# A two-layer decoder trunk on one core: layer 0's gate sums all on VectorE, all 256-column softmax scalings on ScalarE, and a new order of all instructions

## The chip, the cores and the metric

The kernel runs on one core of a Trainium2 chip. The core has five engines that matter here: TensorE (PE, with its weight loads PEld), VectorE (DVE), ScalarE (ACT), GpSimd (POOL) and SyncE (SP), which issues most DMA transfers. Each engine works through its own queue of instructions in order, and waits on semaphores for the others. The metric is the time of one execution in microseconds (us). Three runs of the kernel before had a median of 307.33 us (306.77 to 308.2).

## The reference

The reference is a trunk of two layers over 256 tokens of width 1024, in fp32. A vector `c` sets shift, scale and gate of each layer:

```python
c_act = jax.nn.silu(c)
for layer in range(DEPTH):
    ada = jnp.einsum('bd,de->be', c_act, w_ada[layer]) + b_ada[layer]
    shift, scale, gate = jnp.split(ada, 3, axis=-1)
    h = rms_norm(x, norm_g[layer]) * (1.0 + scale[:, None, :]) + shift[:, None, :]
    ...
        y = even_mixer(h, w_in_even[i], w_out_even[i], ...)    # layer 0
    ...
        y = odd_mixer(h, w_in_odd[i], w_out_odd[i], cos, sin)  # layer 1
    x = x + gate[:, None, :] * y
return rms_norm(x, final_g)
```

Layer 0 has two groups of eight heads of width 64: A attends within a window of 128 tokens with a sink for each head, B adds three gated branches (compressed keys, selected blocks, window). At 256 tokens all blocks of B are selected and the window covers everything, so both of those branches are plain causal attention with their own keys and values. The compressed keys and values come from blocks of 32 tokens through a small network. Layer 1 has sixteen heads of causal attention. Each output is multiplied by a SiLU gate path before the output projection.

## The kernel before

**Two steps.** The code first records all operations, with what each depends on, and issues none. `Plan.issue` then issues the 3102 operations in the order of the table `ORDER` at the head of the file. Each engine's queue is the part of that list that belongs to it. All instructions of the recorded part so carry the line of `issue`, L251 in the profile, and are told apart by the names of their tiles.

**Projections.** Weights are loaded by SyncE into a ring of five `raw` tiles of 1 MB (128 partitions x 2048 fp32). ScalarE casts 512 columns at a time to fp32r, the high part `whi`, and VectorE subtracts to get the low part `wlo`. Three products make one fp32 product (`mm3`): high by high, high by low, low by high, into a bank `ps_pj`. The input is split the same way (`hhi`, `hlo` for layer inputs, `ghi`, `glo` for the output projection).

**The sums for shift, scale and gate** (`ada_...`) are products of one row vector with 1024 x 3072 weights a layer, and there are two ways for a piece of 512 columns. With a `"v"` in `SS_ON`, `G0_ON` or `G1_ON`, VectorE does it (`ada_sums`): the weights of four k-tiles fill a `raw` tile, VectorE multiplies each with a per-partition scalar from `cz` and adds it up in `acc`, 128x512, eight operations from two tiles, and one product with `ones` sums over the partitions and broadcasts. With a `"p"`, TensorE does it (`ada_rows`), 256 columns at a time: eight products, 32 columns of stationary `cz` each, in the four column groups of the array, then a copy by ScalarE into `asb` and a product with `selbc` that sums the groups and broadcasts. Either way the last step for the gate is an addition into `gate` on VectorE. `ada_gate` chooses:

```python
if n == 2:
    T.matmul(pc, ones, a, start=True, stop=True)
else:
    T.matmul(pc[:, :256], selbc, ada_rows(ada_tile(l, (16 + h, 17 + h))), start=True, stop=True)
gs = gate[:, h * P : (h + 2 * n) * P]
V.tensor_tensor(gs, pc[:, : 256 * n], gs, ALU.add)
```

The bytes from memory are the same either way: 2 MB for 512 columns.

**Attention of layer 0.** `attn_four` takes two pairs of heads (or the two branches of one pair of B): scores of 128 queries by 128 or 256 keys into `ps_s`; on VectorE the masked minimum of the negated scores into `sm` (or a spare part of `bigA`) and `mn`; on ScalarE the exponential with its sum into `den`; on VectorE the reciprocal `rc`; then a scaling of each tile by `rc`, transposes on TensorE, a copy `pT` on ScalarE and the products with the values into `ps_o`. There are six such calls: two for A (`a_quad`) and four for B (`b_pair`). In each, four scalings have 256 columns and four have 128. `ON_ACT` names those (pair, head, tile) that ScalarE does:

```python
if (n, i, t) in ON_ACT:
    A.mul(sms[i][:, a:b], sms[i][:, a:b], rc[:, n, i, t : t + 1])
else:
    V.tensor_scalar(sms[i][:, a:b], sms[i][:, a:b], rc[:, n, i, t : t + 1], None, op0=ALU.mult)
```

**Compress.** The network of the compressed keys and values has 16 products of 32 stationary columns each for k and for v, in the four column groups; their order is that of `ORDER`.

**What sets the order around the change.** The jobs of gate 0 and of layer 1's shift and scale are recorded between the attention calls (`fill`), but where they run is set by `ORDER` alone: the table was written by a search, and no planner runs with the kernel. The five `raw` tiles tie the order together, since SyncE loads into a tile only when the last reader of its former content is done: ScalarE and VectorE for a weight, VectorE for sums of kind `"v"`, TensorE for those of kind `"p"`.

Of the kernel before, what the change touches and what calls it, by code (L numbers as in the profile page):

```python
# [25 lines left out]
G0_ON = "vp"  # L26
# [3 lines left out]
ON_ACT = ((0, 1, 1), (1, 1, 1))  # L30
# [7 lines left out]
0 3 1 8 44 10 4 92 11 37 6 2 12 40 13 90 5 14 89 524 15 93 36 45 16 38 1006 87 17 18 19 57 96 20 88 21 91 58 47 59 22  # L38
23 41 94 72 60 42 7 24 25 39 95 26 61 27 73 28 74 106 29 30 76 75 31 62 97 77 48 63 78 49 32 105 51 64 33 65 98 152 79
34 153 67 52 82 80 50 35 81 107 108 109 110 111 112 113 114 115 116 117 53 118 66 119 120 121 122 123 124 125 126 127  # L40
128 129 130 131 132 133 134 135 136 137 138 83 139 55 68 140 69 84 99 70 150 141 142 144 100 143 151 101 146 168 180
56 102 85 148 174 147 175 169 103 186 71 181 149 165 104 171 86 183 145 172 213 154 166 184 163 224 177 159 164 178
225 179 161 187 214 170 176 157 185 162 192 223 167 173 226 189 216 182 195 227 188 198 215 210 207 204 155 211 228
201 219 205 193 199 160 218 229 230 231 232 233 234 158 235 236 237 238 239 240 241 242 243 244 245 246 156 247 248
190 249 202 217 256 250 200 208 209 222 258 251 191 252 257 203 220 260 194 196 259 253 212 197 206 261 264 293 275
262 281 254 221 267 278 282 255 296 273 323 263 290 271 283 274 276 265 287 269 324 335 294 305 272 284 325 291 279
336 288 280 326 292 268 285 286 308 295 334 309 337 297 314 289 298 266 333 320 315 338 321 317 306 328 322 339 310
302 303 327 304 277 340 311 318 270 341 342 343 344 345 346 347 348 349 329 350 525 360 351 352 299 330 307 353 361
364 354 300 301 331 355 312 356 365 313 357 319 332 316 358 366 397 362 369 398 427 394 367 368 431 400 388 389 359
385 377 382 432 395 391 386 428 375 399 363 387 371 390 430 376 383 392 373 401 378 402 429 424 433 384 412 396 413  # L50
379 526 393 434 418 415 523 380 435 381 409 425 683 436 406 407 403 940 374 437 438 439 440 441 442 443 444 445 446
370 447 448 372 421 449 419 450 426 458 408 416 809 451 414 452 460 422 410 411 453 417 461 420 462 404 464 454 423
496 459 478 473 490 484 463 471 405 475 455 487 479 472 469 488 476 467 465 480 474 491 456 497 466 485 498 468 477
520 489 521 470 502 492 545 499 457 486 936 514 549 503 504 508 500 550 501 530 535 509 547 510 546 493 522 529 515
494 532 548 516 527 495 533 481 599 538 482 483 531 601 505 534 528 600 511 506 543 602 517 507 537 544 512 603 551
557 513 610 614 938 552 553 536 554 611 555 935 558 690 559 612 556 615 937 605 616 542 617 541 563 606 564 565 618
560 613 561 566 562 686 567 568 604 575 569 518 619 691 519 620 624 621 607 622 576 570 577 623 687 578 579 571 580
625 572 633 587 688 588 589 634 590 573 684 574 632 581 591 582 583 608 592 685 626 627 628 540 629 636 810 637 655
638 654 639 584 585 631 656 586 593 630 635 594 595 640 596 597 598 657 646 641 663 642 647 643 662 644 661 648 649
650 645 689 651 692 693 694 539 695 670 658 659 669 939 696 697 664 698 660 941 699 700 811 652 701 702 665 653 666  # L60
703 676 814 704 705 943 706 971 707 668 708 667 709 710 944 46 711 712 975 1011 742 945 743 744 745 942 746 947 946
951 950 752 955 954 748 959 958 948 949 974 952 953 749 973 956 957 1047 960 961 750 972 755 1169 671 816 770 771 772
675 773 1170 1034 962 774 747 672 778 673 43 963 776 812 713 964 780 714 674 715 965 716 751 717 815 718 753 977 976
980 984 966 979 983 677 777 988 978 678 982 987 986 981 754 813 985 990 989 991 756 967 757 817 679 992 680 719 720
721 681 993 968 758 1041 779 994 759 868 969 995 869 1042 782 870 871 996 781 970 997 1255 1003 998 783 1001 1004 1002
999 1747 760 775 761 1000 762 1005 818 1048 819 1008 1007 722 784 723 872 820 1009 1013 785 873 724 1012 1010 876 763
1049 821 1056 822 1057 765 823 725 874 824 726 786 1014 880 878 727 877 1015 787 793 896 1016 897 898 899 879 728 1050
904 825 1017 902 826 729 906 827 1018 900 828 730 764 829 908 830 1051 831 881 1058 832 1019 1043 731 766 767 768 1044
732 733 833 769 1020 903 1106 1045 1107 1108 1109 1052 1110 788 1116 789 875 790 834 54 734 1114 1059 1111 1060 882
1021 1112 835 791 1061 883 1022 885 909 907 1132 792 1133 1134 1046 1135 905 794 901 1138 795 1378 796 1062 1117 836  # L70
910 837 1136 1023 682 1053 1113 735 838 839 1242 1063 840 797 911 841 1064 918 1243 1024 1115 913 842 1065 884 891 843
1025 844 736 1066 1137 912 845 737 1171 846 1067 847 848 1256 886 887 890 888 1140 849 850 1139 1026 851 852 1068 1142
738 919 853 854 1257 855 889 1069 739 856 1070 1054 1172 857 858 892 893 1143 894 609 1027 1055 1177 1178 1141 1179
1180 740 1028 1391 798 799 1118 895 1173 800 1390 801 1258 802 803 1185 804 1119 1029 741 805 1260 914 915 916 1030
859 1071 1264 1183 917 1072 1265 1073 1181 1186 1074 1075 1174 1266 920 1127 921 922 860 1031 1182 861 1187 1462 862
863 1267 1184 1259 864 1268 1377 1269 1076 1188 1077 1032 1270 1461 865 1033 1271 923 1272 1035 1078 1175 1262 1121
806 1036 1037 1261 1038 1039 1203 1204 1144 1205 1176 1206 1209 924 925 926 1211 927 1145 928 1120 929 1153 1392 930
931 1213 1040 1246 1244 1247 1245 1147 1250 807 1248 1207 1251 1249 1263 866 1314 1315 1393 1316 1210 1317 1480 867
1122 1474 1123 1124 1079 1273 1080 1189 1125 1126 1081 1082 1394 1083 1212 1084 1274 1085 1086 1252 1128 1318 1129
1130 1320 1275 1276 1087 1146 1131 1088 1152 1253 1395 1321 1148 1149 1150 1208 1089 1324 1090 1482 1277 1151 1278  # L80
1190 1279 1322 1280 932 1091 1475 1214 1092 1154 1155 1093 1323 1254 1281 1282 1156 1463 1340 1157 1341 1342 1343 1215
1325 1382 1380 1379 1386 1348 1501 1384 1381 1344 1385 1383 1346 1319 1464 1158 1347 1159 1481 1160 1161 1349 1191
1162 1350 1163 1198 1164 1216 1165 1192 1351 1166 1502 1167 1387 1396 1397 1465 1398 1224 1399 1197 1193 1194 1326
# [1273 lines left out]
```

## Time and profile before

| what | value |
|---|---|
| median of three runs | 307.33 us (306.77 to 308.2) |
| the profiled execution, its whole time | 307.55 us |
| its span, from the first to the last instruction | 305.4 us |
| TensorE (PE) busy | 294.5 us, 96% |
| VectorE (DVE) busy | 258.4 us, 85% |
| ScalarE (ACT) busy | 184.3 us, 60% |
| TensorE's granted clock, mean | 0.997 |

The profile is one execution. The busy time of an engine is the union of its records, which overlap a little on VectorE and more on TensorE, so the price of an operation within a full queue is read from one start to the next. The clock column is 1.00 in all stretches that are used below, so no time in them hangs on it. Where a wait is named, the name on the right is what came last.

### The profile page before, as it was taken

The page shows a single profiled execution, that of the slowest core. Times are in us where ns is not written, and L with a number is a line of the kernel's source. Part 1 is how long each engine was busy: PE and PEld are TensorE (multiplying, and loading weights), DVE is VectorE, ACT ScalarE, POOL GpSimd, SP SyncE. Part 2 cuts the span into 40 slices and gives each one's busy share as a digit, 9 for nine tenths or more (in the row PEclk, how much of TensorE's full clock was granted, in tenths as well). Part 3 has the DMA queues.
Part 4 walks back from the last instruction along what each step waited for, and adds up shares of the span by engine and source line. Part 5 has one row for each costly group of instructions (what it writes and reads, how often), then busy time and mean ns, then how long its engine had stood idle before and what let it go on. Part 6 is the DMA issues. An engine that isn't in the chain of part 4 may idle for free.

```text
span 305.4 us, 6362 instructions
## 1 busy us (share of the span) xinstructions
PE 294.5 (96%) x2331; PEld 252.0 (83%) x2331; DVE 258.4 (85%) x703; ACT 184.3 (60%) x483; POOL 11.3 (4%) x36
## 2 busy tenths in 40 slices
PE   8899999999999999999999999999999999999990
PEld 8777788997789787888877899999789989877890
DVE  1388999998899999999989778598857999997783
ACT  3476147876679778882547854264647646873630
POOL 6000000002000000000001000000000000000011
PEclk9999999999999999999999999999999999999998
DMA  8999999986956979489899292968098493151003
GB/s 240 355 364 372 387 402 372 332 261 194 337 194 197 320 260 329 139 246 339 259 274 329 61 328 63 366 206 290 0 277 276 144 298 113 52 225 71 0 9 128
DMA packets 60669, 71.82 MB, mean 235 GB/s; under 512 B 2712, under 2 KB 52320, under 8 KB 60640
## 3 DMA queue, kind: packets, MB, share of 16 engines
q1 hardware_dynamic: 60032, 70.90, 70.1%
q10 hardware_dynamic: 448, 0.48, 0.4%
q8 instruction: 18, 0.29, 0.4%
q0 software_dynamic: 160, 0.05, 0.3%
q14 instruction: 11, 0.09, 0.1%
HBM read 70.38 MB, written 1.05 MB: 234 GB/s over the span
## 4 chain that ended last, share of the span: by engine, by line
PE 84%; ACT 4%; DMA 4%; DVE 3%; issue 2%; SPq 0%; POOL 0%; POOLq 0%; ACTq 0%; DVEq 0%
PE ps_pj L251 49%; PE ps_s L251 12%; PE ps_m L251 8%; PE ps_pt L251 7%; PE ps_o L251 7%; DMA raw<-in_w_in_even_dram 2%; DMA xs<-in_x_dram 2%; ACT whi L251 2%; DVE wlo L251 1%; ACT t L251 1%; DVE xs L251 1%; DVE t L251 1%; ACT bigA L251 1%; SPq L251 0%; ACT hhi L251 0%
## 5 line engine op out<-in xcount | busy, mean ns | idle before, releaser
L251 ACT CAST whi<-raw 128x512 fp32r<-128x512 f32 (+1 forms) x132 | 74.7, 599 | 28.8 <-PE ps_pj L251 17.2
L251 DVE TENSOR_TENSOR wlo<-raw,whi 128x512 fp32r<-128x512 f32 (+1 forms) x116 | 74.0, 659 | 8.9 <-ACT whi L251 8.7
L251 PE MATMUL ps_pj<-hhi,whi 128*128 128x256 f32 x256 | 68.0, 286 | 0.0
L251 PE MATMUL ps_pj<-hhi,wlo 128*128 128x256 f32 x256 | 67.8, 286 | 0.0
L251 PE MATMUL ps_pj<-hlo,whi 128*128 128x256 f32 x256 | 67.3, 283 | 0.0
L251 PEld LDWEIGHTS ps_pj<-hhi,whi 128*128 128x128 f32 x256 | 46.5, 188 | 1.1 <-issue 0.3
L251 PEld LDWEIGHTS ps_pj<-hhi,wlo 128*128 128x128 f32 x256 | 46.3, 188 | 0.6 <-issue 0.3
L251 PEld LDWEIGHTS ps_pj<-hlo,whi 128*128 128x128 f32 x256 | 46.3, 188 | 0.1
L251 DVE SCALAR_TENSOR_TENSOR acc<-raw,cz,acc 128x512 f32<-128x512 f32 x42 | 31.3, 745 | 0.3
L251 ACT ACTIVATE sm<-sm,mn 128x256 f32<-128x256 f32 (+1 forms) x58 | 26.0, 450 | 6.5 <-DVE mn L251 6.4
L251 PE MATMUL ps_pj<-whi,hhi 128*128 128x512 f32 (+2 forms) x72 | 26.0, 375 | 0.8 <-ACT hhi L251 0.8
L251 DVE SCALAR_TENSOR_TENSOR wlo<-raw,whi 128x512 fp32r<-128x512 f32 x32 | 21.2, 686 | 5.1 <-ACT whi L251 5.1
L251 PE MATMUL ps_pj<-wlo,hhi 128*128 128x512 f32 (+2 forms) x72 | 25.3, 377 | 0.0
L251 PE MATMUL ps_pj<-whi,hlo 128*128 128x512 f32 (+2 forms) x72 | 25.0, 369 | 0.0
L251 PE MATMUL ps_pj<-whi,ghi 128*128 128x512 f32 (+1 forms) x56 | 20.8, 375 | 0.0
L251 PE MATMUL ps_pj<-wlo,ghi 128*128 128x512 f32 (+1 forms) x56 | 20.5, 372 | 0.0
L251 ACT COPY pT<-ps_pt 128x384 f32<-128x384 f32 x25 | 11.9, 476 | 14.2 <-PE ps_pt L251 14.2
L251 PE MATMUL ps_pj<-whi,glo 128*128 128x512 f32 (+1 forms) x56 | 20.1, 365 | 0.0
L251 PEld LDWEIGHTS ps_pj<-whi,hhi 128*128 128x128 f32 x72 | 13.4, 188 | 3.5 <-ACT hhi L251 1.4
L251 PE MATMUL ps_pt<-ta,sm 128*128 128x128 f32 x87 | 15.7, 276 | 0.0
L251 DVE TENSOR_TENSOR t<-ps_pj,tb 128x512 f32<-128x512 f32 (+2 forms) x22 | 12.0, 586 | 3.4 <-PE ps_pj L251 3.4
L251 PEld LDWEIGHTS ps_pj<-wlo,hhi 128*128 128x128 f32 x72 | 13.3, 189 | 1.9 <-DVE wlo L251 0.2
(231 smaller groups left out, 613.2 us busy)
## 6 DMA issues: line engine op xcount, KB each, us to landing
raw<-in_w_in_odd_dram SPq DMA_DIRECT2D x16, 1024.0 KB, 7.6
raw<-in_w_ada_dram SPq DMA_DIRECT2D x28, 512.0 KB, 5.7
raw<-in_w_in_even_dram SPq DMA_DIRECT2D x8, 652.0 KB, 7.0
raw<-in_w_in_even_dram SPq DMA_DIRECT2D x5, 1024.0 KB, 9.0
t<-in_w_ada_dram SPq DMA_DIRECT2D x16, 256.0 KB, 6.0
raw<-in_w_out_even_dram SPq DMA_DIRECT2D x4, 1024.0 KB, 5.4
raw<-in_w_out_odd_dram SPq DMA_DIRECT2D x4, 1024.0 KB, 6.3
qT<-in_w_ada_dram SPq DMA_DIRECT2D x12, 256.0 KB, 7.2
```

The lines of the kernel that those rows point to most:

```text
L251: self.ops.append(dict(key=eng.key, deps=deps, fn=lambda: getattr(real, name)(*args, **kw)))
```

## The change

Three things differ. `G0_ON` goes from `"vp"` to `"vv"`: the second half of layer 0's gate is summed by VectorE. `ON_ACT` goes from two entries to four: in all six calls of `attn_four`, ScalarE does all four scalings of 256 columns, so that twelve move there from VectorE. And `ORDER` is another list, of 3090 operations.

```diff
-G0_ON = "vp"
+G0_ON = "vv"
...
-ON_ACT = ((0, 1, 1), (1, 1, 1))
+ON_ACT = ((0, 0, 1), (0, 1, 1), (1, 0, 1), (1, 1, 1))
...
-3093 3094 3095 3068 3097 3096 3098 3100 3099 3101
...
```

On SyncE's list, the loads of both halves of `x` now come first, and the narrow piece (384 columns) of the first weight tile comes behind the first pieces for layer 0's sums; further on, loads are shuffled, with the same bytes in all. The tiled products of v's compress network and those of layer 1's shift and scale stand in pairs of column groups (0 1 0 1 ... 2 3 2 3, and 1 3 1 3 0 2 0 2 in one of the latter two); before, k's stood so, v's not. TensorE's list has 189 changes between fp32 and fp32r, where it had 209.

On TensorE, behind the products of probabilities and values (`ps_o`) of an early quad of layer 0, the list before has the first of the two row products of the gate's second half (`raw_103,cz`, eight products), and scores (`ps_s`) and projections (`ps_pj`) around it:

```order
L251 MATMUL ps_o_96<-pT_128,vb 64x256
L251 MATMUL ps_o_96<-pT_129,vb 64x256
L251 MATMUL ps_o_96<-pT_128,vb 64x128
L251 MATMUL ps_o_96<-pT_129,vb 64x128
L251 MATMUL ps_m_67<-raw_103,cz 32x256 x8
L251 MATMUL ps_s_90<-kTb,qT_97 128x128
L251 MATMUL ps_s_91<-kTb,qT_97 128x128
L251 MATMUL ps_s_90<-kTb,qT_97 128x256
L251 MATMUL ps_s_91<-kTb,qT_97 128x256
L251 MATMUL ps_pt_83<-ta,sm_124 128x128 x3
```

The changed list has there one product of the summed rows with `ones`, between the transposes (`ps_pt`) of two heads:

```order
L250 MATMUL ps_pj_94<-hhi,wlo_114 128x256
L250 MATMUL ps_pj_93<-hhi,wlo_113 128x256
L250 MATMUL ps_pj_94<-hhi,whi_110 128x256
L250 MATMUL ps_pt_83<-ta,sm_124 128x128 x3
L250 MATMUL ps_m_67<-acc_105,ones 128x512
L250 MATMUL ps_pt_83<-ta,sm_125 128x128 x3
L250 MATMUL ps_s_90<-kTb,qT_97 128x128
L250 MATMUL ps_s_91<-kTb,qT_97 128x128
L250 MATMUL ps_s_90<-kTb,qT_97 128x256
L250 MATMUL ps_s_91<-kTb,qT_97 128x256
```

The row products and the products with `selbc` are gone, and the one with `ones` waits for `acc_105`, VectorE's last multiply-add of that gate half.

On VectorE, the same sums stand in the middle of softmax calls. `ISA` is the masked minimum, `acc_105` the sum; `raw_103` and `raw_100` are the two loads of this gate half. The changed list:

```order
L250 TENSOR_SCALAR sm_125<-sm_125,rc_140 128x128
L250 SCALAR_TENSOR_TENSOR acc_105<-raw_100,cz,acc_105 128x512
L250 TENSOR_TENSOR t_89<-t_89,dc_160 128x16x16
L250 RECIPROCAL rc_138<-den_135 128x4
L250 SCALAR_TENSOR_TENSOR acc_105<-raw_100,cz,acc_105 128x512
L250 ISA sm_123,mn_132<-ps_s_91,tb 128x128
L250 ISA mn_132 128x1
L250 SCALAR_TENSOR_TENSOR acc_105<-raw_100,cz,acc_105 128x512
L250 ISA sm_123,mn_132<-ps_s_91,tb 128x256
L250 ISA mn_132 128x1
L250 SCALAR_TENSOR_TENSOR acc_105<-raw_100,cz,acc_105 128x512
L250 TENSOR_SCALAR sm_126<-sm_126,rc_140 128x128
```

In the list before, this place has the sums of layer 1's shift and scale (`raw_101`), and a scaling of 256 columns (`sm_126`):

```order
L251 TENSOR_SCALAR sm_124<-sm_124,rc_140 128x128
L251 TENSOR_SCALAR acc_105<-raw_101,cz 128x512
L251 ISA sm_123,mn_132<-ps_s_91,tb 128x256
L251 ISA mn_132 128x1
L251 TENSOR_SCALAR sm_126<-sm_126,rc_140 128x256
L251 ISA bigA,mn_132<-ps_s_90,tb 128x128
L251 ISA mn_132 128x1
L251 TENSOR_TENSOR wlo_113<-raw_104,whi_109 128x512
L251 SCALAR_TENSOR_TENSOR acc_105<-raw_101,cz,acc_105 128x512
L251 SCALAR_TENSOR_TENSOR oT<-oT,ps_pj_93 128x512
L251 RECIPROCAL rc_138<-den_135 128x4
L251 TENSOR_SCALAR sm_125<-sm_125,rc_140 128x128
```

The four multiply-adds from `raw_100` now stand among the minima of a pair of heads, two of them between the minima of one head, and the 256-column scaling is no longer in the queue.

On ScalarE, the same softmax calls, where `sm_...<-sm_...,rc_...` is a scaling and `pT` a copy of transposed tiles. Before:

```order
L251 COPY pT_128<-ps_pt_83 128x384
L251 ACTIVATE bigA,den_135<-bigA,mn_132 128x128
L251 ACTIVATE sm_125<-sm_125,rc_140 128x256
L251 ACTIVATE bigA,den_135<-bigA,mn_132 128x128
L251 ACTIVATE bigA,den_135<-bigA,mn_132 128x256 x2
L251 COPY pT_129<-ps_pt_83 128x384
L251 CAST whi_109<-raw_104 128x512
L251 ACTIVATE sm_127<-sm_127,rc_140 128x256
```

And in the changed list:

```order
L250 COPY pT_128<-ps_pt_83 128x384
L250 ACTIVATE sm_123<-sm_123,rc_139 128x256
L250 ACTIVATE sm_125<-sm_125,rc_140 128x256
L250 ACTIVATE sm_124<-sm_124,rc_140 128x256
L250 ACTIVATE bigA,den_135<-bigA,mn_132 128x128
L250 COPY pT_129<-ps_pt_83 128x384
L250 ACTIVATE sm_126<-sm_126,rc_140 128x256
L250 ACTIVATE bigA,den_135<-bigA,mn_132 128x128
L250 CAST whi_109<-raw_104 128x512
L250 CAST ghi<-oT 128x512
L250 ACTIVATE sm_127<-sm_127,rc_140 128x256
```

Two scalings have become five within ten instructions, three of them in a row; the cast `whi_109` behind them makes the high part of a weight.

## Rows read from the trace of the kernel before

**Rows 1.** The page's first part (busy time, share of the span and instructions of each engine).
```profile
PE 294.5 (96%) x2331; PEld 252.0 (83%) x2331; DVE 258.4 (85%) x703; ACT 184.3 (60%) x483; POOL 11.3 (4%) x36
```

**Rows 2.** The page's fourth part, the chain of work that ended last, by engine.
```profile
PE 84%; ACT 4%; DMA 4%; DVE 3%; issue 2%; SPq 0%; POOL 0%; POOLq 0%; ACTq 0%; DVEq 0%
```

**Rows 3.** The view by stretches: from and to, length, then busy time and instructions of PE, PEld, DVE, ACT and POOL, TensorE's granted clock, DMA share, GB/s. The second to the fourth stretch run from the first softmax operation on VectorE over the last score stage and the last gated product of layer 0 to the first low part of layer 1's input.
```profile
16.00:64.00 48.00, 46.80 (x329) 39.64 (x330) 43.76 (x93) 28.99 (x69) 0.00 (x0) 1.00 1.06 370
...
71.60:90.00 18.40, 18.18 (x176) 14.48 (x178) 16.27 (x72) 12.50 (x45) 0.62 (x2) 1.00 0.83 267
90.00:142.90 52.90, 52.90 (x461) 42.79 (x458) 52.42 (x184) 42.09 (x133) 0.00 (x0) 1.00 0.77 249
142.90:163.10 20.20, 20.20 (x109) 15.63 (x108) 18.84 (x41) 9.91 (x20) 0.94 (x3) 1.00 0.93 291
163.10:284.00 120.90, 120.90 (x982) 107.90 (x981) 100.73 (x254) 72.09 (x179) 0.67 (x1) 1.00 0.57 187
```

**Rows 4.** The view of waits, VectorE alone, in the three stretches from 71.6 to 163.1 us, one after the other: the waiting tile, what it waited for, us in total, times, longest.
```profile
DVE sm L251 <- PE ps_s L251: 0.8, 1, 0.8
DVE hx L251 <- ACT sm L251: 0.7, 1, 0.7
DVE hg L251 <- ACT th L251: 0.3, 1, 0.3
...
DVE sm L251 <- PE ps_s L251: 0.2, 1, 0.2
...
DVE t L251 <- PE ps_s L251: 0.6, 1, 0.6
DVE shs L251 <- PE ps_m L251: 0.4, 1, 0.4
```

**Rows 5.** The chain of waits from 103 to 122 us, in order of time: start, us, what. `ps_m` x2 is first the product with `ones` over 512 columns (104.83), then the broadcast product of one gate part (112.73); `ps_m` x16 are the two row products of the gate's second half.
```profile
104.83 0.86 PE ps_m L251 x2
...
108.43 1.00 PE ps_m L251 x16
...
112.73 0.43 PE ps_m L251 x2
...
115.98 1.01 PE ps_m L251 x16
```

**Rows 6.** The timeline of TensorE at 84 us: start, us, line, operation, out<-in, tile, elements. `ps_pj` products are fp32r, those of `w2v` fp32.
```profile
84.26 0.39 PE L251 MATMUL ps_pj<-hhi,whi 128*128 128x256 f32 x2
84.49 0.28 PE L251 MATMUL ps_pj<-hlo,whi 128*128 128x256 f32 x1
...
84.74 0.36 PE L251 MATMUL ps_pj<-hhi,wlo 128*128 128x256 f32 x1
84.94 0.33 PE L251 MATMUL ps_m<-w2v,hr 128*128 128x64 f32 x2
```

**Rows 7.** The timeline of VectorE in two places: gate or shift sums and a softmax call.
```profile
88.60 0.48 DVE L251 TENSOR_SCALAR acc<-raw,cz 128x512 f32<-128x512 f32 x1
89.12 1.54 DVE L251 SCALAR_TENSOR_TENSOR acc<-raw,cz,acc 128x512 f32<-128x512 f32 x2
90.58 0.28 DVE L251 CUSTOM_DVE_ANT_0 sm<-ps_s,tb 128x128 f32<-128x128 f32 x1
...
92.04 0.35 DVE L251 TENSOR_SCALAR bigA<-bigA,rc 128x256 f32<-128x256 f32 x1
92.31 0.28 DVE L251 TENSOR_SCALAR sm<-sm,rc 128x128 f32<-128x128 f32 x1
...
102.39 0.75 DVE L251 SCALAR_TENSOR_TENSOR acc<-raw,cz,acc 128x512 f32<-128x512 f32 x1
103.06 0.17 DVE L251 TENSOR_SCALAR dc<-dc 128x16 f32<-128x16 f32 x1
```

**Rows 8.** The view by operation and shape, VectorE from 64 to 145 us: busy time, mean ns of one, idle before. The additions into the gate.
```profile
L251 DVE TENSOR_TENSOR gate<-ps_m,gate 128x256 f32<-128x256 f32 x2 | 0.8, 412 | 0.0
L251 DVE TENSOR_TENSOR gate<-ps_m,gate 128x512 f32<-128x512 f32 x1 | 0.7, 658 | 0.0
```

**Rows 9.** ScalarE: by operation and shape over the span (the copy behind a row product, and from the page's fifth part the copy of transposed tiles, whose last number is the idle time before it and its releaser), and two rows of its timeline, a scaling and what follows.
```profile
L251 ACT COPY asb<-ps_m 128x256 f32<-128x256 f32 x4 | 1.5, 365 | 2.1 <-PE ps_m L251 2.1
...
L251 ACT COPY pT<-ps_pt 128x384 f32<-128x384 f32 x25 | 11.9, 476 | 14.2 <-PE ps_pt L251 14.2
...
85.45 0.49 ACT L251 ACTIVATE sm<-sm,rc 128x256 f32<-128x256 f32 x1
85.85 0.49 ACT L251 ACTIVATE bigA<-bigA,mn 128x256 f32<-128x256 f32 x1
```

**Rows 10.** The timeline of TensorE: the compress products of k and what follows them, then those of v and what follows.
```profile
71.63 2.82 PE L251 MATMUL ps_m<-raw,t 128*32 128x256 f32 x32
74.38 0.48 PE L251 MATMUL ps_s<-kTb,qT 64*128 64x128 f32 x3
...
77.02 2.84 PE L251 MATMUL ps_m<-raw,t 128*32 128x256 f32 x32 [0.19 <-issue]
79.79 0.44 PE L251 MATMUL ps_pt<-ta,t 128*128 128x128 f32 x2
```

**Rows 11.** The view of waits, SyncE's DMA queue over the span: us in total, times, longest.
```profile
SPq L251 <- DVE wlo L251: 68.9, 16, 8.3
SPq L251 <- DVE acc L251: 37.0, 9, 13.6
```

248 rows, old and new, of the table ORDER are left out of this document.

## The prediction

> **What bounds the kernel now.** I read the page's sums first: TensorE is busy 294.5 of 305.4 us, VectorE 258.4, ScalarE 184.3 [rows 1]. The chain of waits agrees, with 84% of it on TensorE and 4% or less on anything else [rows 2]. That share is an average, so I then cut the span into the stages that the change touches: the loads up to 64 us, then layer 0's attention from the first softmax operation on VectorE (71.6 us) to the last gated product (142.9 us), and the output projection up to the first low part of layer 1's input (163.1 us) [rows 3]. The columns to read are the busy times of PE and DVE. TensorE has no gap to speak of from 71.6 to 163.1. VectorE is nearly as full: 52.42 of 52.90 us in the middle stretch, and 87.53 of 91.50 over the three (16.27, 52.42 and 18.84). So two engines stand side by side, and VectorE's whole reserve there is 2.13 + 0.48 + 1.36 = 3.97 us. ScalarE has 27 us free over the same three stretches. Behind 163.1 us VectorE has 20 us of reserve, and nothing there is edited but the order.
>
> The waits of VectorE name 3.0 of those 3.97 us [rows 4]: three are for scores or projections from TensorE (0.8, 0.2, 0.6), one for layer 1's shift product (0.4), and two for ScalarE in the small compress chain (0.7, 0.3). A shorter list on TensorE can close the first kind, but not the last.
>
> **The change, part by part.** *Gate sums off TensorE.* The second half of the gate leaves two row products of eight tiled multiplications each. On the chain they stand as 1.00 and 1.01 us, each with nothing around it [rows 5]. With them go two broadcast products of 0.43 each, and one ones-product over 512 columns comes, like the one that took 0.86: even. TensorE: -2.0 us.
>
> *Fewer changes between fp32 and fp32r on TensorE.* I counted them in the two lists: 209 before, 189 after. Within a run of fp32r products, two took 0.23 from the start of the first to the start of what follows (84.26 to 84.49), so 0.12 each; a single one between two fp32 products took 0.20 [rows 6]. That is 0.08 for one change. Twenty times 0.08 is 1.6 if every change costs that, 0.8 if only the entry into one kind does; I take 1.3. TensorE's stream is then 3.3 us shorter, with 2.8 and 3.6 as ends.
>
> *Gate sums onto VectorE.* They add one scaling and seven multiply-adds of 128x512. Records overlap on VectorE, so I take starts, not durations: 0.52 from the scaling (88.60) to the next start, 0.73 each for the two multiply-adds behind it (1.46 from 89.12 to 90.58), 0.67 for another (102.39 to 103.06) [rows 7]. With 0.69 they come to 4.8 + 0.5 = 5.3. Two gate additions of 0.41 become one of 0.66, which is -0.2 [rows 8].
>
> *Softmax scalings off VectorE.* Six calls of four heads move two 256-column scalings each: twelve. Start to start one takes 0.27 (92.04 to 92.31) [rows 7]: -3.2. A rope addition over 256 columns and a small copy also leave this stretch in the new order, -0.4. VectorE's list from the first softmax to layer 1's first low part: 5.3 - 0.2 - 3.2 - 0.4 = +1.5 us.
>
> *Onto ScalarE.* The same scaling there is 0.49 long, 0.40 from start to start (85.45 to 85.85) [rows 9]. Twelve are +4.8, and two copies of 0.37 go: +4.1. The 27 us free hide it in sum. What could show is position: the third fence of the change has five scalings within ten instructions of ScalarE's queue, and behind a late one wait transposed copies and casts, for which TensorE waits. If one pile of three stood in the open, 1.2 us would be lost. In the trace of before it is ScalarE's copies of transposed tiles that wait for TensorE, 14.2 us over the span [rows 9], so I take 0.2 and keep 1.2 for the range.
>
> *Tiled products in pairs.* The compress products of k stand in pairs of column groups before already, those of v do not (groups 1 0 0 0 3 3 0 2 2 3 ...). From their start to the next kind of product they took 2.75 and 2.77 us [rows 10]: nothing is to be had, and I put 0. The eight shift-and-scale products of layer 1 go the other way, from a turn over four groups to pairs in one of their two visits: 1.00 for eight products in such turns [rows 5] against 1.38 for eight in pairs, half of 2.75, so up to +0.4 on TensorE, in a stretch where it has company. I put 0.1 of it into the net. The Trainium skill, TensorEngine Tiling (Array Packing), section Key Properties under Tiling Modes, says that tiles operate independently and that different ones can load weights and multiply in parallel. By it v's order, with five neighbours in one group, should have been slower than k's pairs by some of those five (an estimate from the rows: 5 x 0.17, up to 0.9 us); rows 10 show 0.02, so the measurement decides, and by the rule TensorE's stream would be -4.2 instead of -3.3, with the same limit from VectorE.
>
> *The start.* The order of the first loads changes, the bytes do not, and the stage up to 64 us runs on them: a DMA share of 1.06 at 370 GB/s [rows 3]. A piece of 256 KB more or less ahead of the first product is 0.7 us either way; I take 0.
>
> *Sum.* TensorE alone would end the three stretches 3.3 us earlier, at 88.2 instead of 91.5. VectorE cannot: 87.53 busy plus 1.5 is 89.0, so with no idle time left the gain is 2.5. Idle time will be left: the waits for ScalarE and for the shift product (0.7 + 0.3 + 0.4) stay, and with the two lists now equally long neither can run ahead to cover the other's order. In before, VectorE was ahead of what TensorE next asked for; in the new list the distance between a pair's scores and its transposes on TensorE is shorter through the middle quads. From 3.97 us of idle I let 3.0 close; gain 3.0 - 1.5 = 1.5, less 0.2 (ScalarE) and 0.1 (pairs): -1.2 us. The profiled execution took 307.55 (span 305.4 and 2.1 around it), so 306.35, and it was 0.22 above the median of the runs: **306.1 us**.
>
> The ends: no idle closes, +1.5, with the ScalarE pile +2.7 (310.0); all idle closes, -2.5 (304.8); TensorE's gain kept whole because the new order hands VectorE work on past 163.1 us, -3.3 (304.0).
>
> **Rivals.** *B, TensorE's gain arrives nearly whole, 304.0 to 305.0.* For it: 96% busy on TensorE, and the 20 us of reserve behind 163.1 us, into which low parts of weights could slide. Against it: 52.42 of 52.90 on VectorE. Adding up VectorE's list with these prices to the same gated product in both orders, it comes there 3.3 us earlier at the first of layer 0, 5.4 later at the second and 2.1 later at the last, so the reserve would have to lie in the right places.
>
> *C, the exchange cancels, 307.0 to 308.0.* What leaves TensorE comes back as waits for VectorE: only 1.5 of the 3.97 us closes, against 1.5 of new work. For it: VectorE in the middle stretch has 0.48 us to give. Against it: four of the six named waits are for TensorE, which gets faster.
>
> *D, slower, about 310.* Eight multiply-adds read two raw buffers that TensorE's row products used to release. Five such buffers feed all weights, in SyncE's order, and its queue already waits 37.0 us for gate and shift sums (nine times, 13.6 at most) and 68.9 for low parts [rows 11]. If one wait of the mean, 37.0 / 9 = 4.1 us, is added on a weight that is needed at once, casts and TensorE stop behind it: -1.2 + 4.1 = +2.9, 310.2. It decides from the point where a load lands later than its cast is due. Against it: TensorE has no gap over the three stretches of before [rows 3], although these queues wait all along.
>
> *E, the list does not bring what its counts say:* the 20 changes between fp32 and fp32r cost nothing where TensorE's pipeline hides them, and the pairs nothing either. TensorE is then 2.0 us shorter, at 89.5 of 91.5, which is longer than VectorE's 89.0; the three waits for ScalarE and the shift product (1.4) come on top of part of it: about -0.7, 306.6. This lies inside the forecast's range, and I give it 0.1 of the chance there.
>
> **How the numbers follow.** My forecast, A, 305.2 to 306.9 with E in it: 0.46. B 0.22, C 0.20, D 0.12. A measurement of this kernel tells 0.5% from no change, so faster is below 305.8 and slower above 308.9. All of B and two fifths of A are faster: 0.40; the rest of A and C 0.47; D with a little of C's far end 0.13. The range for 8 in 10 leaves out D and half of B's low end: 304.2 to 308.4.
>
> **What would show it.** In the profile after: the two row products and broadcasts gone from the chain, one ones-product of 0.86 in the attention; VectorE's busy time over the attention and the output projection up by about 1.5 (703 instructions to 698 over the span); TensorE's busy time down by about 3, but with new gaps of some 2 us named as waits for VectorE between the softmax calls; SyncE's waits for sums longer. Wrong would be: TensorE still without a gap (B), waits for casts or loads behind 90 us (D), or a stage up to 64 us that is more than 0.7 us off.

## The result and the profile after

The changed kernel takes 306.68 us, the median of 20 runs (305.59 to 308.45); the kernel before, run in the same rounds, 308.56 (306.77 to 310.57). The ratio is 0.9943, with a 95% interval of 0.9923 to 0.9963: 1.8 us faster, 1.1 to 2.4. The forecast was -1.2 us from 307.33, or 306.1 us, with a range of 304.2 to 308.4. Before's 20 runs lie 1.2 us above the three that were shown first, so the time came 0.6 us above the forecast and the gain 0.6 above it too; the runs on the start, below, show why. What follows goes by differences, and by what each stretch of the traces lost or won. Two slow executions are left out of the ratios below, 311.01 us with the old start and 478.63 us with the sums alone.

The profiled execution of the changed kernel took 306.25 us, with a span of 304.4. Its page, engines and chain, which answer to [rows 1, 2]:

```profile
PE 293.0 (96%) x2297; PEld 251.7 (83%) x2297; DVE 258.5 (85%) x698; ACT 188.2 (62%) x493; POOL 12.2 (4%) x36
...
PE 81%; DMA 11%; DVE 3%; issue 1%; SPq 1%; ACT 0%; POOLq 0%; POOL 0%; DVEq 0%; ACTq 0%
```

TensorE is 1.5 us less busy, VectorE unchanged over the span, ScalarE 3.9 more (4.1 was worked out). The stretches, at the same times as in [rows 3]:

```profile
71.60:90.00 18.40, 18.16 (x176) 13.75 (x172) 17.04 (x82) 14.92 (x56) 0.53 (x1) 1.00 0.96 316
90.00:142.90 52.90, 52.90 (x430) 43.50 (x428) 52.76 (x170) 43.47 (x131) 0.00 (x0) 1.00 0.73 240
142.90:163.10 20.20, 18.83 (x109) 14.68 (x111) 18.23 (x39) 10.37 (x22) 1.46 (x3) 1.00 0.80 249
```

VectorE is busy 52.76 of 52.90 us in the middle. TensorE is still busy for all 52.90 of them, with 430 records where it had 461: the edit itself takes 34 off its list (2331 to 2297), so the count is no sign of waiting. From 142.9 to 163.1 us it has a gap of 1.37 us that was not there before.

To place the difference I take three marks on TensorE: the first compress product, the end of the last value products of layer 0 (from there 24 products of the output projection run without a break), and the last product of the output projection's second half. The chain of waits of before, at the second mark:

```profile
140.15 1.88 PE ps_o L251 x20
142.03 5.79 PE ps_pj L251 x24
```

and of the changed kernel:

```profile
137.94 1.88 PE ps_o L250 x20
139.82 5.79 PE ps_pj L250 x24
```

The timeline of TensorE at the first and third mark, before:

```profile
162.90 0.40 PE L251 MATMUL ps_s<-whi,glo 128*128 128x512 f32 x1
```

and after, with v's compress products, now in pairs, and what follows them:

```profile
70.91 2.82 PE L250 MATMUL ps_m<-raw,t 128*32 128x256 f32 x32
...
76.09 2.82 PE L250 MATMUL ps_m<-raw,t 128*32 128x256 f32 x32
78.84 0.44 PE L250 MATMUL ps_pt<-ta,t 128*128 128x128 f32 x2
...
162.23 0.47 PE L250 MATMUL ps_s<-whi,glo 128*128 128x512 f32 x1
```

With 71.63 for before's first compress product [rows 10], the attention from the first to the second mark took 70.40 us before and 68.91 after: 1.5 us won. From the second to the third it was 20.87 and 22.41: 1.5 us given back, of which the gap is 1.37 and one product of layer 1 that now runs ahead of the mark about 0.3. The start won 0.7. Behind the third mark the two executions differ by 0.3 us.

**The gap.** TensorE's timeline after, then SyncE's DMA issues, then the view of the issues between 146.7 and 149 us (operation, count, KB each, us to landing):

```profile
156.51 1.07 PE L250 MATMUL ps_m<-raw,cz 128*32 128x256 f32 x16 [1.37 <-DVE xs L250]
```

```profile
146.80 0.37 SPq L250 DMA_DIRECT2D raw<-in_w_in_odd_dram  x1
147.21 1.14 SPq L250 DMA_DIRECT2D raw<-in_w_ada_dram  x2
148.60 0.88 SPq L250 DMA_DIRECT2D raw<-in_w_in_odd_dram  x1
```

```profile
raw<-in_w_in_odd_dram SPq DMA_DIRECT2D x2, 1024.0 KB, 10.5
raw<-in_w_ada_dram SPq DMA_DIRECT2D x2, 256.0 KB, 8.5
```

The row names VectorE's residual addition `xs` as the releaser, but that addition ended 0.84 us earlier, and the product doesn't read `xs`. It reads `raw`, and the last piece of that was issued at 147.8, between two loads of 1 MB, and landed 8.7 us later, at 156.42, 0.09 us ahead of the product. In the three other traces in which this product waits (the changed kernel's second, the one with more work on TensorE, and the one with the scalings undone) it starts 0.09 us behind the landing as well. In before the last piece landed at 154.0, and the same row product stood at 155.7 without a gap.

### The profile page after: what moved, and what is told of

Read it like the earlier page. It is cut to its first block, busy times and chain, and to the rows that moved or that the text cites. A ratio compares the mean times of both kernels' runs of the same rounds, so it can differ in the third digit from the quotient of the medians.

```text
span 304.4 us, 6282 instructions
## 1 busy us (share of the span) xinstructions
PE 293.0 (96%) x2297; PEld 251.7 (83%) x2297; DVE 258.5 (85%) x698; ACT 188.2 (62%) x493; POOL 12.2 (4%) x36
## 4 chain that ended last, share of the span: by engine, by line
PE 81%; DMA 11%; DVE 3%; issue 1%; SPq 1%; ACT 0%; POOLq 0%; POOL 0%; DVEq 0%; ACTq 0%
PE ps_pj L250 52%; PE ps_s L250 11%; PE ps_o L250 7%; PE ps_pt L250 7%; PE ps_m L250 6%; DMA qT<-in_w_ada_dram 4%; DMA raw<-in_w_in_even_dram 3%; DMA gate<-in_w_ada_dram 2%; DMA t<-in_w_ada_dram 2%; DVE xs L250 1%; DVE bigA L250 1%; SPq L250 1%; DVE t L250 1%; DVE sm L250 0%; ACT t L250 0%
## 5 line engine op out<-in xcount | busy, mean ns | idle before, releaser
L250 DVE TENSOR_TENSOR wlo<-raw,whi 128x512 fp32r<-128x512 f32 (+1 forms) x116 | 73.1, 657 | 6.4 <-ACT whi L250 6.1
L250 DVE SCALAR_TENSOR_TENSOR acc<-raw,cz,acc 128x512 f32<-128x512 f32 x49 | 36.4, 742 | 0.2
L250 PE MATMUL ps_pj<-whi,hhi 128*128 128x512 f32 (+2 forms) x72 | 25.1, 370 | 0.0
L250 PE MATMUL ps_pt<-ta,sm 128*128 128x128 f32 x87 | 16.3, 276 | 0.0
L250 PEld LDWEIGHTS ps_pj<-whi,hlo 128*128 128x128 f32 x72 | 13.3, 188 | 1.9 <-issue 0.3
```

What stands on the lines that cost most here:

```text
L250: self.ops.append(dict(key=eng.key, deps=deps, fn=lambda: getattr(real, name)(*args, **kw)))
```

## Experiments

Twelve runs follow: ten kernels, one of them twice, and the changed kernel once more; each is compared with the kernel before on the same chip. A ratio less one, times 308.6 us, gives the microseconds. The runs came in three groups on three chips, and the changed kernel stood beside the last group only: the scalings undone, the old start and the second run of the moved loads. Elsewhere, "slower than the changed kernel" sets a ratio against its 0.9943, which was not measured beside it. Its second ratio was 0.9960, so such a difference can be off by half a microsecond.

**The new start alone.** The first 657 operations in the changed list's order, the others as before.

```diff
-0 3 1 8 44 10 4 92 11 37 6 2 12 40 13 90 5 14 89 524 15 93 36 45 16 38 1006 87 17 18 19 57 96 20 88 21 91 58 47 59 22
+0 3 1 8 37 7 10 2 1006 11 40 89 12 43 4 13 92 42 524 14 87 5 15 94 16 44 93 36 17 6 18 38 45 19 88 41 20 90 47 21 91
...
```

> The kernel before, with only the first 657 operations (to about 62 us) in the changed list's order: loads, splits and first projections; all else is as before. Theory S (the new start is worth what the two traces show at the first compress product, 71.63 before and 70.91 after): 0.7 us faster than before, 0.4 to 1.0, and the first compress product near 70.9. Theory N (the two starts differ by one execution's chance, since the bytes are the same): within 0.3 us of before.

Ratio 0.9972 (0.9948 to 0.9995): 0.9 us faster, 0.2 to 1.6, as theory S has it. But the profiled execution has its first compress product at 71.66, level with before's and not near 70.9: in that pair of executions the start won nothing. The reverse, and the clocks on record, show how both can be true.

**The changed kernel with the old start.**

```diff
-0 3 1 8 37 7 10 2 1006 11 40 89 12 43 4 13 92 42 524 14 87 5 15 94 16 44 93 36 17 6 18 38 45 19 88 41 20 90 47 21 91
+0 3 1 8 44 10 4 92 11 37 6 2 12 40 13 90 5 14 89 524 15 93 36 45 16 38 1006 87 17 18 19 57 96 20 88 21 91 58 47 59 22
...
```

> The changed kernel with its first 657 operations in the order of before. Theory S (the new start is worth about 0.9 us, as it was worth in the list of before): 0.5 to 1.3 us slower than the changed kernel, first compress product later than 71.2 us. Theory N: within 0.3 us of it.

Ratio 0.9966 (0.9940 to 0.9992), where the changed kernel itself had 0.9943 and, on the same chip as this one, 0.9960: slower than it by 0.7 us by the one and by 0.2 by the other, inconclusive by the times. The traces say more. Over all kernels that ran, the first compress product came at 70.8 to 71.7 us in the eight with the new start, and at 71.5, 71.6, 72.0, 72.7, 74.0 and 74.6 in the six with the old. The last three of these have something in common. TensorE's timeline in one of them, the kernel before with more work on VectorE, which differs from before only behind the compress products:

```profile
8.33 0.27 PE L251 MATMUL ps_s<-ta,t 128*128 128x128 f32 x1
10.78 0.33 PE L251 MATMUL ps_pj<-ta,t 128*128 128x128 f32 x1 [2.18 <-DVE t L251]
```

and its stretches (columns as in [rows 3]):

```profile
8.00:12.00 4.00, 1.82 (x15) 1.40 (x14) 0.80 (x3) 2.75 (x6) 0.57 (x1) 0.99 0.96 324
12.00:16.00 4.00, 4.00 (x57) 3.69 (x59) 1.90 (x6) 0.11 (x1) 0.00 (x0) 0.58 1.07 392
```

In the old list the second half of `x` is loaded behind a piece for the sums, TensorE stands 2.18 us for it, and in the next stretch the granted clock is 0.58, partly at the lower level of 1.2 GHz. The three late starts have 0.58, 0.60 and 0.69 there, behind waits of 2.18, 2.06 and 2.23 us; the three others have 1.00, behind waits of 1.29 to 1.59. In the new start both halves of `x` are loaded first, TensorE's wait at this place is 0.53 us at most, and all eight traces have 1.00. The changed kernel:

```profile
9.27 0.33 PE L250 MATMUL ps_s<-ta,t 128*128 128x128 f32 x1 [0.52 <-DVE t L250]
```

The delay comes with the drop: the 48 row products with `qT` that follow begin at 12.89 us in before and at 14.27 in the trace with more work on VectorE. Behind it the loads fall back too: from 16 to 20 us they run at 244 to 299 GB/s in the three late traces and at 350 to 390 in the three others.

So the start's gain is mostly that a late start no longer happens in some executions. The mean granted clock, which is on record for every execution here, bears this out. It is 0.984 to 0.989 in the three late traces and 0.994 to 0.997 in the three others of the old start, so I take 0.991 or less as the sign of a late start where there is no trace. Of the 91 executions of before that ran beside these kernels, 44 have that sign, with a mean of 309.6 us, and 47 don't, with a mean of 307.9; of all 96 executions with the new start, two have it. The new start alone has a mean of 307.7 us, and before's executions without the sign on its chip 307.8. By this reading a late start costs before about 1.8 us and comes in about half of its executions, and without one the two starts are level. Before's first profile, at 0.997, was one without it, and its first three times, 1.2 us under the later median, fit that. What the rest of the change is worth can be read where no late start plays a part: on the chip that ran both, before's 23 executions without the sign have a mean of 308.0 us and the changed kernel's ten 306.8, which is 1.2 us less.

**The scalings alone, in the old list.**

```diff
-ON_ACT = ((0, 1, 1), (1, 1, 1))
+ON_ACT = ((0, 0, 1), (0, 1, 1), (1, 0, 1), (1, 1, 1))
```

> The kernel before in its own order, with only the twelve softmax scalings of 256 columns moved to ScalarE. VectorE's list in the attention gets 3.2 us shorter, TensorE's stays. Theory V (TensorE is the bound there, VectorE close behind): 0.2 to 1.0 us faster, by what closes of TensorE's waits and VectorE's idle time moves up. Theory Q (position in ScalarE's queue decides): copies and casts come late in a list not written for it, 0.5 to 1.5 us slower, with waits of TensorE for pT or whi.

Ratio 1.0033 (1.0005 to 1.0061): 1.0 us slower, 0.2 to 1.9. Theory Q. The view of waits, TensorE's weight loads from 60 to 175 us, has a line that before's had not at that size:

```profile
PEld ps_pt L251 <- ACT bigA L251: 1.5, 5, 0.5
```

Transposes wait for ScalarE's scaling of `bigA`. The attention ends at 143.69, 71.70 us after the first compress product, 1.3 more than in before.

**The scalings undone, in the new list.**

```diff
-ON_ACT = ((0, 0, 1), (0, 1, 1), (1, 0, 1), (1, 1, 1))
+ON_ACT = ((0, 1, 1), (1, 1, 1))
```

> The changed kernel with the two-of-four scalings of before: the same list, but twelve scalings of 256 columns back on VectorE, which gets 12 x 0.27 = 3.2 us longer in the attention. Theory C (VectorE sets the end there): 2.5 to 4 us slower than the changed kernel. Theory P (TensorE does): under 1 us slower.

Ratio 1.0041 (1.0020 to 1.0061), 1.3 us slower than before and 2.5 slower than the changed kernel on the same chip: theory C, at its lower end. The attention took 71.93 us, 3.0 more than 68.91, nearly all of the 3.2 that were put back on VectorE. The list was not written for these scalings, so their places in it have a part in this. TensorE's busy column (stretches as in [rows 3]) shows little of it, 71.17 of 71.94 us:

```profile
70.76:142.70 71.94, 71.17 (x596) 56.00 (x594) 70.53 (x258) 54.30 (x172) 0.52 (x1) 1.00 0.75 247
```

The records of neighbouring products overlap, so waits shorter than the overlap leave no gap. From one start to the next they do show: the 88 score products of the attention take 11.0 us here and 9.7 in the changed kernel.

**The sums alone, in the old list.** They have a tile of their own there, since `acc` is taken by layer 1's sums.

```diff
-G0_ON = "vp"
+G0_ON = "vv"
...
-                a = sb([P, 512], "acc", 1)
+                a = tb[:, 512:1024] if fn is ada_gate and l == 0 and i == 1 else sb([P, 512], "acc", 1)
```

> The kernel before in its own order with only the gate's second half moved to VectorE: eight sums, four before each place where a row product stood, one per four VectorE operations, in a tile of their own (the rope tables' tile, free by then; the load that refills that tile comes behind the last sum). TensorE minus 2.0 us, VectorE plus 5.1 in the attention. Theory V (VectorE takes back what it has no room for; 4 us of idle time in the three stretches): 0.5 to 3 us slower than before, with new waits of TensorE for mn, rc or oT. Theory T (TensorE alone is the bound): 2 us faster.

Ratio 1.0131 (1.0087 to 1.0175): 4.0 us slower, 2.7 to 5.4. Theory V, and more than its upper end in the middle of the interval. TensorE's waits:

```profile
PE ps_s L250 <- DVE mn L250: 3.7, 2, 3.1
```

Scores wait for a bank that VectorE's minimum has not read yet, behind the sums. The two edits so cost 1.0 and 4.0 us each in a list that wasn't written for them; the whole change, with its own list, is 1.8 us faster.

**Which engine sets the end.** Four kernels put 1.8 us more onto one engine in the attention, in before and after: sixteen transposes or three subtractions issued twice. For before the last two lines name other instructions.

```diff
-            self.ops[i]["inst"] = self.ops[i]["fn"]()
+            for _ in range(2 if i in (1250, 1254, 1492) else 1):
+                self.ops[i]["inst"] = self.ops[i]["fn"]()
```

> The kernel before, with sixteen transposes of softmax tiles issued twice, spread over the attention of layer 0: TensorE plus 16 x 0.11 = 1.8 us, nothing else (the second writes the same numbers). Theory P (TensorE is the bound of before, with no gap from 71.6 to 163.1 us): 1.6 to 2.0 us slower than before. Theory V (VectorE is): under 0.6.

Ratio 1.0065 (1.0032 to 1.0099), 2.0 us slower than before; the attention took 72.10 us, 1.7 more. Theory P.

> The kernel before, with three subtractions that make low parts of weights issued twice, spread over the attention: VectorE plus 3 x 0.61 = 1.8 us, nothing else. Theory P (VectorE has 4 us of idle time in the three stretches and stands ahead of TensorE): 0 to 0.8 us slower. Theory V: 1.8.

Ratio 1.0052 (1.0018 to 1.0086), 1.6 us slower, though theory P had at most 0.8. By the marks, the attention took 72.35 us, 1.95 more than in before, with new waits of TensorE for VectorE. VectorE's idle time elsewhere was no reserve for the middle stretch. The two ratios of before also hold different numbers of late starts (nine of twelve executions, and four of twelve). Among the executions without that sign, the one with more on TensorE is 1.5 us slower than before (three executions) and the one with more on VectorE 1.8 (eight).

> The changed kernel with the same sixteen transposes issued twice: TensorE plus 1.8 us. Theory C (after the change VectorE sets the end of the attention, TensorE has room behind it): 0 to 1.0 us slower than the changed kernel, so 0.8 to 1.8 faster than before. Theory P (TensorE is still the bound): 1.6 to 2.0 slower than the changed kernel, about level with before.

Ratio 0.9981 (0.9956 to 1.0006), 1.2 us slower than the changed kernel by the middle values; the attention took 70.44 us, 1.5 more, with no wait of TensorE in it. Theory C had at most 1.0, theory P at least 1.6: neither, and nearer to P by the attention.

> The changed kernel with three subtractions of low parts issued twice: VectorE plus 1.8 us in the attention, where it has 0.14 us of idle time in 52.9. Theory C: 1.4 to 2.0 us slower than the changed kernel, level with before. Theory P: 0 to 0.6 slower.

Ratio 1.0027 (0.9997 to 1.0057), 2.6 us slower than the changed kernel by the middle values, more than theory C's 2.0; the attention took 2.2 more. TensorE's waits from 71 to 150 us, none of which the changed kernel shows:

```profile
PE ps_pj L250 <- DVE oT L250: 0.7, 2, 0.5
PE ps_s L250 <- DVE mn L250: 0.6, 1, 0.6
PE ps_s L250 <- ACT whi L250: 0.5, 1, 0.5
```

Taken together: in both kernels, work added to either engine in the attention is paid nearly in full. TensorE's added work is paid without a new wait in the attention, so its own list sets the pace there before and after. VectorE's is paid through new waits of TensorE: at the three places tried, VectorE has no room in either list.

**The late load.** Two issues moved on SyncE's list, 1595 and 1567, the small pieces, ahead of 1736, the load of 1 MB.

```diff
-1651 1617 1736 1629 1559 1613 1595 1546 1560 1567 1615 1552 1652 1630 1624 1587 1631 1804 1561 1622 1621 1632 1633
+1651 1617 1595 1567 1736 1629 1559 1613 1546 1560 1615 1552 1652 1630 1624 1587 1631 1804 1561 1622 1621 1632 1633
```

> The changed kernel with two DMA issues moved on SyncE's list: the last pieces for layer 1's shift and scale (256 KB each, into raw tiles that are free) ahead of the 1 MB weight load that they stood behind. Theory L (the 1.37 us in which TensorE stands before the row product at 156.5 us is the wait for that load, issued at 148 and landed 8.4 to 8.7 us later): 1.0 to 1.4 us faster than the changed kernel, 2.7 to 3.3 faster than before. Theory X (it is the residual addition xs on VectorE, which the trace names): the same as the changed kernel, 1.5 to 2.2 faster than before.

Ratio 0.9921 (0.9892 to 0.9950), 2.4 us faster than before, between the two theories. The gap before the row product is gone. In its place, in this trace, TensorE stands at the second half of the output projection, and ScalarE for its weights:

```profile
146.88 0.50 PE L250 MATMUL ps_s<-whi,ghi 128*128 128x512 f32 x1 [1.29 <-ACT whi L250]
```

```profile
146.20 2.71 ACT L250 CAST whi<-raw 128x512 fp32r<-128x512 f32 x5 [2.35 <-DMA raw<-in_w_out_even_dram]
```

That load was issued at 138.47, as in the changed kernel, where it took 5.2 us to land; here it took 7.7. The same wait of TensorE, 1.22 us, stands in the trace with the old start, whose loads aren't moved. So two loads are due at this place with little to spare, and which of them is late differs between executions. A second run, beside the changed kernel on one chip:

> The changed kernel with the two small loads ahead of the 1 MB load, once more. Theory L (the late small load costs the list about a microsecond): 0.7 to 1.4 us faster than the changed kernel on the same chip. Theory W (the output projection waits for loads anyway, here for the last weights of the output projection, issued at 138.5 us in both): within 0.4 us of the changed kernel, with a wait for whi or raw in place of the one removed.

Ratio 0.9951 (0.9926 to 0.9976), with neither wait in its trace: the second to the third mark took 21.1 us.

> The changed kernel once more, unchanged, so that a second trace of it and times on the same chip as the next three are there. 0.4 to 0.8% faster than before. If the wait of 1.37 us before the row product of layer 1's shift and scale belongs to the list, it stands here again, at 0.5 us or more; if it was one execution's chance, it does not.

Ratio 0.9960 (0.9936 to 0.9984), 1.2 us faster than before. The gap is there again, but smaller, just under the 0.5 that was named:

```profile
155.97 1.07 PE L250 MATMUL ps_m<-raw,cz 128*32 128x256 f32 x16 [0.44 <-issue]
```

The attention took 68.92 us, within 0.01 of the first trace. On the same chip the moved loads are thus worth 0.3 us by the middle values, with intervals that overlap by far: that the row product waited for the load is shown by its landing, 0.09 us ahead of the product in each of four traces, but that moving it makes the kernel faster is not shown. It is faster than before in both runs, like the changed kernel.

## Why the prediction was right, and where not

**Direction and size: right, by another way than the sum's.** 1.2 us were forecast, 1.8 measured (1.1 to 2.4), and the time lies inside the range. The sum had 0 for the start and 1.2 for the rest. About 0.9 of the 1.8 belong to the start; the rest, where no late start plays a part, is about 1.2 as forecast, but two of its terms were wrong and made up for each other, which is luck, and it holds a late load of 0.4 to 1.4 us, which the sum put at nothing.

**"TensorE's stream is then 3.3 us shorter": mis-sized, 1.5 in the attention.** The row products' 2.0 are gone, and the ones-product that stands for two broadcasts of 0.43 is in the chain after at its forecast 0.86, in place of [rows 5]:

```profile
99.89 0.86 PE ps_m L250 x2
...
109.18 0.86 PE ps_m L250 x2
```

But the attention took only 1.5 us less, so its other products, the same in both lists but for two, took 0.5 us more. From start to start, the projection products take 0.8 us less, the transposes 0.6 more and the small products 0.8 more. The forecast had put 1.3 on twenty fewer changes between fp32 and fp32r; twelve of these lie in the attention, and no net gain shows there. The price of 0.08 for a change looked at one side only. Three transposes take 0.24 us from their start to the next product where that is an fp32r one (first pair, before), and 0.33 where it is an fp32 one (second pair, after):

```profile
96.25 0.49 PE L251 MATMUL ps_pt<-ta,bigA 128*128 128x128 f32 x3
96.49 0.36 PE L251 MATMUL ps_pj<-hlo,whi 128*128 128x256 f32 x1
...
108.69 0.49 PE L250 MATMUL ps_pt<-ta,sm 128*128 128x128 f32 x3
109.02 1.02 PE L250 MATMUL ps_m<-acc,ones 128*128 128x512 f32 x2
```

The 0.08 that the first fp32r product takes more is thus given back by a transpose ahead of it, and 23 of the 43 such changes in before's attention stand behind transposes. This is what rival E named, a list that doesn't bring what its counts say; its price was 0.7 us. What the rest of the 0.5 us is made of stays open.

**VectorE as the limit ("VectorE cannot", gain 1.5): not shown.** The forecast's 1.5 is TensorE's 3.3 less what VectorE holds back. Its own sign for that, gaps of some 2 us named as waits for VectorE, is missing: TensorE has no wait in the attention of the changed kernel, in two traces alike (68.91 and 68.92 us), and SyncE's waits for sums got shorter, 16.3 us for 37.0, not longer. The 88 scores take 9.69 us from start to start in both kernels, and the 112 products with the values 10.43. So TensorE's list got 1.5 us shorter and all of that arrived; that the forecast also had 1.5 is luck. A part of the 0.5 may still be waits too short to show. What does hold of this step is that VectorE has no room to give: without the scalings moved the attention takes 3.0 us longer, and with the sums alone, in the old list, the kernel takes 4.0.

**"From 3.97 us of idle I let 3.0 close": wrong as a step.** By the same stretches VectorE's idle time is 1.36 + 0.14 + 1.97 = 3.47 us after, so 0.5 closed. VectorE's part of the gain came the way that rival B named, by work handed on: its last gated product starts 71.35 us after the first compress product, where it was 71.23.

```profile
142.26 0.42 DVE L250 SCALAR_TENSOR_TENSOR oT<-ps_o,oT 128x256 f32<-128x256 f32 x1
```

VectorE didn't get faster. But TensorE ends the last value products 2.44 us ahead of it, where it was 0.83 ahead, and has 5.79 us of output projection to do that don't need this product. The kernel before with 1.8 us more on VectorE paid 1.6 (0.6 to 2.7) although VectorE had 4 us idle over the three stretches: idle time counted as a reserve only where it lay.

**"The start ... I take 0": wrong.** It is worth 0.9 us in the old list (0.2 to 1.6), half of the whole gain, and by its middle value outside the 0.7 either way that was worked out from one piece at 370 GB/s. By the means, it is worth nothing between executions without a late start, so the step fits the one trace that it was read from, and not the kernel. It asked how many bytes came first; the trace of before had the answer's other half, a wait of TensorE for the second half of `x`, and I didn't look for it. What a longer wait there brings with it, the lower clock, was not in that execution.

**ScalarE's pile, 0.2 with 1.2 at most: in the new list not separable, in the old list 1.0.** The list has to be written for it.

**Rival D, a late load: its mechanism is real, at a tenth to a third of its price.** 0.44 and 1.37 us of TensorE, not 4.1, and by another way than the eight sums: TensorE now comes to the output projection earlier, and the last piece for the row product lands later, at 156.4 us where it was 154.0, among loads of 1 MB. "TensorE has no gap over the three stretches of before" was no argument against it.

**Pairs, 0:** v's products took 2.75 us from their start to the next kind of product where they took 2.77, so nothing, as forecast. The 0.4 that pairs could cost in layer 1's row product didn't come: it stands at 1.07 in both traces, and at 1.00 in before.

## What to carry to other kernels

Where two engines are both full, price an edit on both, the one that gets the work and the one that loses it, and test with a little added work on each: here both paid in full, each edit alone cost time in the old list, and together they paid in a list made for them. Price a change of kind from the start of the product ahead of it, not only by the product behind it. Read waits from start to start, since a busy column can hide short ones. Count idle time as a reserve only in the stretch where the new work falls, and ask of a stage that is reached earlier whether its loads come earlier too. Compare starts over several executions before calling them equal: one profile can be the lucky one, and the clock of each run tells which.

## What was not expected of the hardware

TensorE's granted clock in the first 16 us differs between executions of the same instructions. In the old list TensorE waited 1.29 to 2.23 us for the second half of `x`. The product behind the wait started at 10.2 to 10.9 us in all six traces; what differed is how early TensorE had come there, at 8.2 to 8.6 us in the three with the longest waits and at 8.7 to 9.3 in the others. In the three with the longest waits the clock was 0.58 to 0.69 from 12 to 16 us, and the first compress product came at 72.7 to 74.6 instead of 71.5 to 72.0 us. The first fp32r product behind a transpose takes 0.20 us where the next takes 0.12, but the transpose ahead of it takes 0.03 where the one before takes 0.11, so the change is free there. And a load of 1 MB, issued at the same 138.47 us from the same list, landed after 5.2 us in one execution and 7.7 in another.
